# Mixture-of-experts layer: one capacity of 152 slots against eight capacities from 152 to 120, with the experts put in order on the chip

## The chip, the cores and the metric

The kernel runs on one core of a Trainium2 chip, as one program. The metric is the device time of one execution in microseconds (us). Three runs of the kernel before gave 4085.41, 4088.22 and 4089.95 us; the median is 4088.22 us. The execution that the profiler recorded took 4086.74 us.

## The reference, cut to what matters

Two transformer blocks run one after the other on 512 tokens of width 1024. The first has two layers; the second of these ends in a mixture of experts (MoE), which is the only part that changes:

```python
logits = (xt @ w_router).astype(jnp.float32)          # 512 tokens x 8 experts
top_logits, top_idx = lax.top_k(logits, TOP_K)        # TOP_K = 2
gates = jax.nn.softmax(top_logits, axis=-1)
order = jnp.argsort(top_idx.reshape(-1))              # 1024 (token, expert) pairs, sorted by expert
xs = xt[order // TOP_K]
hid = silu(ragged_dot(xs, w_gate, group_sizes)) * ragged_dot(xs, w_up, group_sizes)
ys = ragged_dot(hid, w_down, group_sizes)             # 1024 -> 3584 -> 1024 for each expert
out = einsum('nk,nkd->nd', gates, y)                  # y: ys put back into the tokens' order
```

So 1024 pairs are spread over 8 experts by the data. For the inputs of this kernel, worked out from the reference, the eight experts get 137, 118, 116, 149, 142, 117, 118 and 127 pairs (in the order of their numbers, 0 to 7).

## The kernel before

The reference's group sizes are known only at run time, while the program's shapes are fixed. So every expert gets `CAP` = 152 places ("slots") for its pairs; 8 x 152 = 1216 slots serve 1024 pairs. A fallback (`moe_overflow`) treats pairs that find no slot; it stands behind a branch on a flag, `anyo`, and is skipped if every expert's count is at most 152.

**Routing.** `moe_ranks` takes the two best experts of each token, counts with small matmuls how many earlier pairs chose the same expert (`pr`; its last row block holds the totals of the experts), and makes of it the flag and each pair's row `pos` in a buffer in DRAM (expert times 152 plus rank). `moe_route` builds expert 0's input on TensorE from a selection matrix `first`, and scatters all scaled token rows to the buffer `xg` by indirect DMAs on GpSimd.

**The expert loop** (`for e in range(NE)` in `moe`) runs the experts in the order of their numbers. For each of them `prep` loads its 152 rows (128 and 24), transposes both pieces and splits them into a rounded part and a remainder: `xhl` holds the two side by side, `xb` is a bf16 copy. Then come 14 chunks of two weight tiles each (`moe_w_gate`, `moe_w_up`, 1 MB a tile), and 16 tiles of `moe_w_down` (0.9 MB): 44 tiles an expert, 352 in all. A weight tile passes four stations (`wload_b`): a DMA issued by SP into one of five `wraw` buffers; a copy on ScalarE (ACT) to the rounded part `wh`; a subtraction on VectorE (DVE) that leaves the remainder `wl` in bf16 and frees the `wraw` buffer; and TensorE (PE), which holds 128 columns of the tile as stationary weights while the tokens stream past. There are four pairs of `wh` and `wl`. In `wh` matmuls 2 x 152 = 304 columns stream (rounded part and remainder of the tokens at once), in `wl` matmuls 152. ACT and DVE also take every result out of PSUM, on tiles of 152 or 304 columns: L935 to L946 for gate and up, L972 to L981 for down.

**The last expert** does not go through DRAM: `moe_select` makes a matrix that sends its slots to tokens, and L988 and L989 add its output to the tokens (`cb`, once for the first 128 slots and once for the other 24). At the same time GpSimd gathers the other experts' outputs and adds them (`gather_add`).

**Order.** Each engine's instruction list is put in order at build time by a scheduler that simulates the program with its own costs; tiles carry the waits. ACT, DVE and SP work off their lists in order. The weight tiles' place among the PSUM work on ACT and DVE is therefore set by that simulation, not by what the chip does.

Of the kernel before, what the change touches and what calls it, by code (L numbers as in the profile page):

```python
# [23 lines left out]
S = 512  # L24
# [4 lines left out]
CAP = 152  # L29
OVR = 384  # L30

BASE = 2 * S
HID = (8, 8, 6, 6)
# [18 lines left out]
def _constants():  # L52
# [41 lines left out]
    c["iota8"] = np.tile(np.arange(8, dtype=np.float32), (128, 1))  # L94
# [4 lines left out]
class K:  # L99
# [705 lines left out]

    def moe_begin(self, psum, h):
# [16 lines left out]
        self.iota8 = self.const("iota8", [128, 8])  # L823
# [22 lines left out]
    def moe(self, h):  # L846
        tc, nc, a = self.tc, self.nc, self.a
        C, C2 = CAP, CAP - 128
        NF = 28
        with ExitStack() as c:  # L850
# [10 lines left out]
            flags = ph.tile([1, NE * 3], I32, name="flags")  # L861
# [11 lines left out]
            def parts():  # L873
                return work.tile([128, ND, 2, C], FR, name="xhl"), work.tile([128, ND, C], BF, name="xb")
# [8 lines left out]
            def prep_first():  # L883
                x = parts()
                for d in range(ND):
                    ps = psum.tile([128, C], F, name="tr", bufs=2)
                    for t in range(NT):
                        nc.tensor.matmul(ps, h[:, t, d * 128:(d + 1) * 128], first[:, t], start=t == 0, stop=t == NT - 1)
                    split(d, ps, *x)
                return x  # L890

            def prep(e):
                xr = work.tile([128, D], F, name="xr", bufs=1)
                xr2 = work.tile([C2, D], F, name="xr2", bufs=1)
                ld = [nc.scalar.dma_start(xr, xg[BASE + e * C:BASE + e * C + 128]),
                      nc.scalar.dma_start(xr2, xg[BASE + e * C + 128:BASE + (e + 1) * C])]
# [4 lines left out]
                x = parts()  # L901
                for d in range(ND):
                    ps = psum.tile([128, C], F, name="tr", bufs=2)
                    nc.tensor.transpose(ps[:, :128], xr[:, d * 128:(d + 1) * 128], self.ident)
                    nc.tensor.transpose(ps[:, 128:], xr2[:, d * 128:(d + 1) * 128], self.ident[:C2, :C2])
                    split(d, ps, *x)
# [7 lines left out]
            for e in range(NE):  # L914
                if e == 1:
                    order.close()
                xhl, xb = nxt
                hid = [work.tile([128, n, 2, C], FR, name=f"hid{i}", bufs=1) for i, n in enumerate(HID)]
                hb = [work.tile([128, n, C], BF, name=f"hb{i}", bufs=1) for i, n in enumerate(HID)]
                at = [(i, j) for i, n in enumerate(HID) for j in range(n)]  # L920
                for ch in range(NF // 2):
                    sums = []
                    for name in ("moe_w_gate", "moe_w_up"):
                        wh, wl = ready.pop(0) if ready else self.wload_b(a[name][e, ch], 2048)
                        wh = wh.rearrange("p (d c) -> p d c", d=ND)
                        wl = wl.rearrange("p (d c) -> p d c", d=ND)
                        t = work.tile([128, 2, C], F, name=name[-4:])
# [22 lines left out]
                else:  # L950
                    sel = self.moe_select(work, psum, pos, gates, BASE + (NE - 1) * C)
                    self.gather_add(work, h, yg, pos, gates, BASE + (NE - 1) * C)
# [4 lines left out]
                yr2 = work.tile([C2, D], F, name="yr2", bufs=1)  # L957
                for d in range(ND):
                    ps = psum.tile([128, 2, C], F, name="mm", bufs=4)
                    for half in range(2):  # L960
                        wh, wl = self.wload_b(a["moe_w_down"][e, d, half], 1792)
# [9 lines left out]
                    t = work.tile([128, C], F, name="yt")  # L971
# [3 lines left out]
                    nc.tensor.transpose(pt[:, 0], t[:, :128], self.ident)  # L975
                    nc.tensor.transpose(pt[:C2, 1], t[:, 128:], self.ident)
                    ds = slice(d * 128, (d + 1) * 128)
                    y1 = work.tile([128, 2, C], F, name="w_up")[:, 0, :128] if last else yr[:, ds]
                    y2 = yr2[:, ds]
                    nc.scalar.activation(y1, pt[:, 0], AF.Copy)  # L980
                    nc.scalar.activation(y2, pt[:C2, 1], AF.Copy)  # L981
                    if last:
# [14 lines left out]
                if not last:  # L997
                    nc.scalar.dma_start(yg[BASE + e * C:BASE + e * C + 128], yr)
                    nc.scalar.dma_start(yg[BASE + e * C + 128:BASE + (e + 1) * C], yr2)
# [4 lines left out]
    def moe_select(self, work, psum, pos, gates, row0):  # L1004
        nc = self.nc
        C2 = CAP - 128
        it = self.iota_cap
# [3 lines left out]
        out = [work.tile([128, S], F, name="xr", bufs=1), work.tile([C2, S], F, name="xr2", bufs=1)]  # L1011
        for t in range(NT):
            one = [work.tile([128, CAP], F, name="yt") for _ in range(2)]
# [4 lines left out]
            nc.tensor.transpose(pt[:, 0], one[0][:, :128], self.ident)  # L1018
            nc.tensor.transpose(pt[:C2, 1], one[0][:, 128:], self.ident)
            ts = slice(t * 128, (t + 1) * 128)  # L1020
            nc.vector.tensor_copy(out[0][:, ts], pt[:, 0])
            nc.vector.tensor_copy(out[1][:, ts], pt[:C2, 1])
        return out

# [38 lines left out]
    def moe_ranks(self, pre, psum, flags, anyo, rstd, pos):  # L1063
# [14 lines left out]
        nc.vector.tensor_tensor(oh, self.iota8[:, None, None, :].to_broadcast(ohs), idf[:, :, :, None].to_broadcast(ohs),  # L1078
# [1100 lines left out]
```

## Time and profile before

| | |
|---|---|
| median of three runs | 4088.22 us |
| profiled execution | 4086.74 us |
| its span, first to last instruction | 4084.9 us |
| TensorE busy | 3862.3 us, 95% of the span |
| VectorE busy | 2884.7 us, 71% |
| ScalarE busy | 2162.8 us, 53% |
| data moved | 888.86 MB, mean 218 GB/s |
| expert loop | about 1102 to 2345 us of the span |

The shares of busy time are means over stages of very different kinds. The loop over the experts is about three tenths of the span, and it can be read by itself: windows of 148 us, cut at the starts of the experts, show each of them apart. [...] "DMA share" is the mean busy share of the 16 DMA engines.

### The profile page before, as it was taken

The page shows a single profiled execution, that of the slowest core. Times are in us where ns is not written, and L with a number is a line of the kernel's source. Part 1 is how long each engine was busy: PE and PEld are TensorE (multiplying, and loading weights), DVE is VectorE, ACT ScalarE, POOL GpSimd, SP SyncE. Part 2 cuts the span into 40 slices and gives each one's busy share as a digit, 9 for nine tenths or more (in the row PEclk, how much of TensorE's full clock was granted, in tenths as well). Part 3 has the DMA queues.
Part 4 walks back from the last instruction along what each step waited for, and adds up shares of the span by engine and source line. Part 5 has one row for each costly group of instructions (what it writes and reads, how often), then busy time and mean ns, then how long its engine had stood idle before and what let it go on. Part 6 is the DMA issues. An engine that isn't in the chain of part 4 may idle for free. (4 is left out here: it accounts for less than half of the span.)

```text
span 4084.9 us, 64628 instructions
## 1 busy us (share of the span) xinstructions
PE 3862.3 (95%) x25939; PEld 3477.4 (85%) x25940; DVE 2884.7 (71%) x4529; ACT 2162.8 (53%) x3554; POOL 605.3 (15%) x380
## 2 busy tenths in 40 slices
PE   8999999999799999999998999998889799799998
PEld 7887887999699999999997887688888799688886
DVE  4655543455388888888889658459998776677776
ACT  4332223655387777778776655533335587333333
POOL 0000000000100000000006000003444543432231
PEclk9999999999899999999999999799999899899999
DMA  4344543121489889888887521026886855899995
GB/s 135 101 135 166 186 148 107 62 77 47 161 286 321 309 298 318 306 302 311 305 303 293 189 73 57 2 104 226 292 294 233 297 185 204 311 354 335 336 338 195
DMA packets 222254, 888.86 MB, mean 218 GB/s; under 512 B 20904, under 2 KB 82105, under 8 KB 169338
## 3 DMA queue, kind: packets, MB, share of 16 engines
q1 hardware_dynamic: 102034, 640.55, 44.8%
q0 software_dynamic: 40608, 146.24, 9.9%
q10 hardware_dynamic: 79304, 97.86, 7.0%
q8 instruction: 206, 3.38, 0.3%
q14 instruction: 102, 0.84, 0.1%
HBM read 810.62 MB, written 72.38 MB: 216 GB/s over the span
## 5 line engine op out<-in xcount | busy, mean ns | idle before, releaser
L1033 DVE TENSOR_TENSOR wl<-wraw,wh 128x2048 bf16<-128x2048 f32 (+1 forms) x352 | 782.3, 2222 | 189.9 <-ACT wh L1032 188.9
L1032 ACT ACTIVATE wh<-wraw 128x2048 fp32r<-128x2048 f32 (+1 forms) x352 | 647.1, 1838 | 249.9 <-PE mm L932 118.8
L151 DVE TENSOR_TENSOR wl<-wraw,wh 128x2048 fp32r<-128x2048 f32 (+1 forms) x219 | 522.9, 2388 | 245.5 <-ACT wh L150 237.6
L150 ACT ACTIVATE wh<-wraw 128x2048 fp32r<-128x2048 f32 (+1 forms) x219 | 415.4, 1897 | 455.0 <-PE mm L157 208.9
L932 PE MATMUL mm<-xhl,wh 128*128 128x304 f32 x3584 | 617.3, 314 | 16.1 <-DVE gate L936 8.0
L932 PEld LDWEIGHTS mm<-xhl,wh 128*128 128x128 f32 x3584 | 514.9, 190 | 20.2 <-DVE w_up L936 9.6
L158 PE MATMUL mm<-xh,wl 128*128 128x384 f32 (+1 forms) x1088 | 373.6, 349 | 50.6 <-DVE wl L151 50.6
L156 PE MATMUL mm<-xh,wh 128*128 128x384 f32 (+1 forms) x1088 | 378.8, 350 | 8.4 <-ACT wh L150 6.9
L157 PE MATMUL mm<-xl,wh 128*128 128x384 f32 (+1 forms) x1088 | 378.2, 348 | 0.0
L934 PE MATMUL mm<-xb,wl 128*128 128x152 bf16 x3584 | 315.1, 231 | 0.0
L1703 POOL DMA_INDIRECT row<-in_peer_u_rows,eidx x128 | 199.3, 1557 | 694.2 <-DVE pv L1727 494.5
L157 PE MATMUL acc<-wl,ah 128*128 128x512 f32 x768 | 297.8, 397 | 1.8 <-DVE wl L151 1.8
L156 PE MATMUL acc<-wh,ah 128*128 128x512 f32 x768 | 270.0, 396 | 23.6 <-ACT ah L2013 23.6
L965 PE MATMUL mm<-hid,wh 128*128 128x304 f32 x1792 | 285.4, 309 | 0.0
L158 PE MATMUL acc<-wh,al 128*128 128x512 f32 x768 | 282.6, 397 | 0.0
L934 PEld LDWEIGHTS <-wl 128*128 128x128 bf16 x3584 | 229.2, 98 | 38.8 <-issue 0.7
L158 PEld LDWEIGHTS mm<-xh,wl 128*128 128x128 f32 x1088 | 209.7, 193 | 58.8 <-DVE wl L151 56.1
L965 PEld LDWEIGHTS mm<-hid,wh 128*128 128x128 f32 x1792 | 254.5, 189 | 0.4
L1703 POOL DMA_INDIRECT row<-in_peer_v,eidx x128 | 177.1, 1384 | 365.2 <-DVE h L1904 318.2
L156 PEld LDWEIGHTS mm<-xh,wh 128*128 128x128 f32 x1088 | 210.3, 193 | 14.1 <-ACT wh L150 8.8
L157 PEld LDWEIGHTS mm<-xl,wh 128*128 128x128 f32 x1088 | 210.3, 193 | 2.8
L156 PEld LDWEIGHTS acc<-wh,ah 128*128 128x128 f32 x768 | 145.0, 189 | 58.9 <-ACT ah L2013 23.8
(587 smaller groups left out, 8302.1 us busy)
## 6 DMA issues: line engine op xcount, KB each, us to landing
wraw<-in_moe_w_gate SPq DMA_DIRECT2D x112, 1024.0 KB
wraw<-in_moe_w_up SPq DMA_DIRECT2D x112, 1024.0 KB
wraw<-in_moe_w_down SPq DMA_DIRECT2D x128, 896.0 KB
wraw<-in_peer_u SPq DMA_DIRECT2D x64, 1024.0 KB
wraw<-in_peer_v SPq DMA_DIRECT2D x64, 1024.0 KB
wraw<-in_w_ada SPq DMA_DIRECT2D x24, 1024.0 KB
G<-gst SPq DMA_DIRECT2D x6, 4096.0 KB
gw<-G ACTq DMA_DIRECT2D x64, 384.0 KB
```

Of the source, the lines that this page charges most:

```text
L150: nc.scalar.activation(wh[:, :n], raw[:, :n], AF.Copy)
L151: nc.vector.tensor_sub(wl[:, :n], raw[:, :n], wh[:, :n].bitcast(F))
L156: mm(out, ah, bh, start=start, stop=False)
L157: mm(out, ah, bl, start=False, stop=False)
L158: mm(out, al, bh, start=False, stop=stop)
L932: nc.tensor.matmul(ps, wh[:, d, fs], xhl[:, d], start=d == 0, stop=False)
L934: nc.tensor.matmul(ps[:, 0], wl[:, d, fs], xb[:, d], start=False, stop=d == ND - 1)
L965: nc.tensor.matmul(ps, wh[:, fs], hid[at[ft][0]][:, at[ft][1]], start=ft == 0, stop=False)
L1032: nc.scalar.activation(wh[:, :n], raw[:, :n], AF.Copy)
L1033: nc.vector.tensor_sub(wl[:, :n], raw[:, :n], wh[:, :n].bitcast(F))
L1703: self.tc.keep_in_program_order(nc.gpsimd.indirect_dma_start(out=r, out_offset=None, in_=table, in_offset=bass.IndirectOffsetOnAxis(ap=eid ...
```

## The change

The eight capacities are now 152, 152, 144, 136, 132, 128, 124 and 120 (sum 1088), and belong to places in the order of work, not to experts. Expert 0 always has the first place. The other seven are put in order on the chip by their counts, the largest first, with DVE operations in `moe_ranks` that compare all counts with each other; from that come each expert's capacity and its first row. The list of experts by place (`eid`) is read by SP into registers, and from the second place on SP's weight DMAs take their address from such a register. All shapes of a place follow its capacity; places with at most 128 slots have no second piece of rows, so their second transposes and copies go, and in the last place the second half of `cb` goes. Buffers keep their sizes. The fallback gets a wider buffer and four blocks an expert instead of three; it runs only if a count is over its place's capacity. Sorted, the counts above are 137 (expert 0), 149, 142, 127, 118, 118, 117 and 116.

```diff
-CAP = 152
+CAPS = (152, 152, 144, 136, 132, 128, 124, 120)
+CAP = CAPS[0]
+START = [sum(CAPS[:i]) for i in range(NE + 1)]
...
             def prep(e):
-                xr = work.tile([128, D], F, name="xr", bufs=1)
-                xr2 = work.tile([C2, D], F, name="xr2", bufs=1)
+                C, row = CAPS[e], BASE + START[e]
+                n, C2 = min(C, 128), max(C - 128, 0)
+                xr = work.tile([128, D], F, name="xr", bufs=1)[:n]
+                ld = [nc.scalar.dma_start(xr, xg[row:row + n])]
+                if C2:
+                    xr2 = work.tile([CAP - 128, D], F, name="xr2", bufs=1)[:C2]
...
             for e in range(NE):
+                C, row = CAPS[e], BASE + START[e]
+                n1, C2 = min(C, 128), max(C - 128, 0)
+                if e:
+                    ev = nc.values_load(self.eid[0:1, e:e + 1], engines=(mybir.EngineType.SP,), min_val=0, max_val=NE - 1)
...
+                def of_expert(name, *at):
+                    if e == 0:
+                        return a[name][(0,) + at]
+                    return a[name][(bass.ds(ev, 1),) + at].rearrange("o p c -> (o p) c")
...
-                        wh, wl = ready.pop(0) if ready else self.wload_b(a[name][e, ch], 2048)
+                        wh, wl = ready.pop(0) if ready else self.wload_b(of_expert(name, ch), 2048)
-                        t = work.tile([128, 2, C], F, name=name[-4:])
+                        t = work.tile([128, 2 * CAP], F, name=name[-4:])[:, :2 * C].rearrange("p (f c) -> p f c", f=2)
...
-                            nc.tensor.matmul(ps[:, t], sel[0][:, ts], y1, start=True, stop=False)
-                            nc.tensor.matmul(ps[:, t], sel[1][:, ts], y2, start=False, stop=True)
+                            nc.tensor.matmul(ps[:, t], sel[:, ts], y1, start=True, stop=True)
...
     def moe_ranks(self, pre, psum, flags, anyo, rstd, pos):
-        fl = pre.tile([1, 3, NE], F, name="fl")
-        for q in range(3):
-            nc.vector.tensor_scalar(fl[:, q], pr[0:1, NT], float(CAP + 128 * q), None, op0=OP.is_gt)
+        key = pre.tile([128, 8], F, name="key")
+        nc.vector.scalar_tensor_tensor(key, pr[:, NT], 8.0, after, op0=OP.mult, op1=OP.add)
+        nc.vector.tensor_tensor(gt, key[:, None, :].to_broadcast(sq), key[:, :, None].to_broadcast(sq), op=OP.is_gt)
+        nc.vector.tensor_reduce(place, gt, axis=AX.X, op=OP.add)
+        nc.vector.tensor_tensor(at, i8[:, None, :].to_broadcast(sq), place[:, :, None].to_broadcast(sq), op=OP.is_equal)
+        cap, begin = pick(caps, "ecap"), pick(starts, "ebeg")
+        nc.vector.tensor_tensor(gt, at, i8[:, :, None].to_broadcast(sq), op=OP.mult)
+        nc.vector.tensor_reduce(ef, gt.rearrange("p e q -> p q e"), axis=AX.X, op=OP.add)
+        nc.vector.tensor_copy(self.eid, ef[0:1])
+        nc.vector.tensor_tensor(past, pr, cap[:, None, :].to_broadcast([128, NT + 1, 8]), op=OP.subtract)
+        fl = pre.tile([1, 4, NE], F, name="fl")
+        for q in range(4):
+            nc.vector.tensor_scalar(fl[:, q], past[0:1, NT], float(128 * q), None, op0=OP.is_gt)
...
```

Two places show what this does to the order. The first is SP's list at the start of expert 0, just behind the branch over the fallback. Before, the weight loads stand one behind the other:

```order
L868 ISA x2
L1030 DMA wraw<-in_moe_w_gate 128x2048
L1030 DMA wraw<-in_moe_w_up 128x2048
L1030 DMA wraw<-in_moe_w_gate 128x2048
L1030 DMA wraw<-in_moe_w_up 128x2048
L1030 DMA wraw<-in_moe_w_gate 128x2048
```

Now seven pairs of these rows, one pair for each later place (two pairs are shown), stand between the third and the fourth load:

```order
L874 ISA x2
L1050 DMA wraw<-in_moe_w_gate 128x2048
L1050 DMA wraw<-in_moe_w_up 128x2048
L1050 DMA wraw<-in_moe_w_gate 128x2048
L933 TENSOR_LOAD eid
L933 ISA x2
L933 TENSOR_LOAD eid
L933 ISA x2
```

So all seven register loads have moved ahead of the fourth weight load; in the later places each weight load has one more row, an `ISA`, ahead of it, for its address. The second place is DVE's list in the middle of the last expert's gate and up part, about its 21st weight tile. Before, a weight tile (`wl`) stands between the two halves of the PSUM work (`gate` or `w_up` from `mm`) of the tile before:

```order
L1033 TENSOR_TENSOR wl<-wraw,wh 128x2048
L936 TENSOR_TENSOR gate<-mm,gate 128x152
L946 TENSOR_TENSOR hid_25528<-gate,hid_25528 128x2x152
L936 TENSOR_TENSOR w_up<-mm,w_up 128x152
L1033 TENSOR_TENSOR wl<-wraw,wh 128x2048
L936 TENSOR_TENSOR w_up<-mm,w_up 128x152
L936 TENSOR_TENSOR gate<-mm,gate 128x152
L941 TENSOR_TENSOR gate<-gate,w_up 128x304
L1033 TENSOR_TENSOR wl<-wraw,wh 128x2048
```

Now it stands behind both halves of `w_up`:

```order
L1053 TENSOR_TENSOR wl<-wraw,wh 128x2048
L960 TENSOR_TENSOR w_up<-mm,w_up 128x120 x2
L965 TENSOR_TENSOR gate<-gate,w_up 128x240
L1053 TENSOR_TENSOR wl<-wraw,wh 128x2048
L960 TENSOR_TENSOR gate<-mm,gate 128x120
L970 TENSOR_TENSOR hid_26438<-gate,hid_26438 128x2x120
L960 TENSOR_TENSOR gate<-mm,gate 128x120
L1053 TENSOR_TENSOR wl<-wraw,wh 128x2048
```

Counted over the whole list, a weight tile's subtraction in a gate and up part stood 4.5 tiles ahead of the PSUM work before, in every expert. Now it stands 4.5 ahead in the places up to the fifth, 4 in the seventh, and 2 in the middle of the last one.

## Rows read from the trace of the kernel before

**Rows 1.** Windows: expert 1, then expert 7's two parts (columns as named).

```profile
core 0: us, PE busy (x) PEld busy (x) DVE busy (x) ACT busy (x) POOL busy (x), PEclk, DMA share, GB/s
1262.00:1410.00 148.00, 148.00 (x1383) 140.38 (x1381) 124.19 (x145) 115.57 (x183) 0.00 (x0) 1.00 0.88 308
2149.00:2268.00 119.00, 101.87 (x904) 93.96 (x903) 114.32 (x128) 77.94 (x128) 69.90 (x32) 0.97 0.78 283
2268.00:2336.00 68.00, 68.00 (x558) 60.67 (x556) 38.84 (x40) 46.47 (x134) 0.55 (x1) 1.00 0.49 172
```

**Rows 2.** Windows of line L932 alone: PE busy (count), PEld, clock, DMA.

```profile
1705.00:1853.00 148.00, 76.61 (x448) 64.03 (x448) 1.00 0.89 308
```

**Rows 3.** Waits, 1300 to 2000 us: total, times, longest.

```profile
DVE wl L1033 <- ACT wh L1032: 113.3, 191, 2.1
ACT wh L1032 <- PE mm L932: 73.3, 131, 0.9
```

**Rows 4.** Timeline of PE, gate and up: start, duration of the row, count.

```profile
1605.58 1.36 PE L932 MATMUL mm<-xhl,wh 128*128 128x304 f32 x8
1606.78 0.70 PE L934 MATMUL mm<-xb,wl 128*128 128x152 bf16 x8
1607.28 1.36 PE L932 MATMUL mm<-xhl,wh 128*128 128x304 f32 x8
```

**Rows 5.** Timeline of PE, another layer, 256 columns streaming.

```profile
1068.04 0.28 PE L157 MATMUL mm<-wl,nxh 128*128 128x256 f32 x1
1068.16 0.28 PE L158 MATMUL mm<-wh,nxl 128*128 128x256 f32 x1
```

**Rows 6.** Timeline of PE, the second block, 128 columns streaming.

```profile
3098.40 0.27 PE L1850 MATMUL ps<-gha,ghb 128*128 128x128 f32 x1
3098.51 0.28 PE L1851 MATMUL ps<-ghl,ghb 128*128 128x128 f32 x1
```

**Rows 7.** Timeline, the counting matmuls of the routing, then a DVE operation there.

```profile
1083.09 0.49 PE L1085 MATMUL mm<-both,low 128*128 128x8 bf16 x14 [2.29 <-DVE both L1081]
1083.85 0.20 DVE L1096 TENSOR_TENSOR oh<-oh,mm 128x64 f32<-128x64 f32 x1
```

**Rows 8.** Windows with the DMA engines nearly full, columns as in Rows 1.

```profile
2148.00:2160.00 12.00, 12.00 (x117) 11.43 (x115) 10.20 (x14) 9.00 (x15) 0.57 (x1) 1.00 0.99 357
3700.00:3800.00 100.00, 100.00 (x430) 80.48 (x429) 76.13 (x60) 31.86 (x24) 27.10 (x24) 1.00 0.96 335
```

**Rows 9.** Lines by shape, 1853 to 2000.8 us (expert 5): busy, mean ns.

```profile
L1033 DVE TENSOR_TENSOR wl<-wraw,wh 128x2048 bf16<-128x2048 f32 x29 | 66.5, 2293 | 13.3 <-ACT wh L1032 13.3
L936 DVE TENSOR_TENSOR w_up<-mm,w_up 128x152 f32<-128x152 f32 x28 | 8.7, 309 | 0.0
L941 DVE TENSOR_TENSOR gate<-gate,w_up 128x304 f32<-128x304 f32 x14 | 6.5, 468 | 0.1
L1032 ACT ACTIVATE wh<-wraw 128x2048 fp32r<-128x2048 f32 x29 | 55.6, 1917 | 17.3 <-PE mm L932 12.5 <-PE mm L965 4.9
L976 PE MATMUL tr<-c_ident,yt 128*24 128x128 f32 x9 | 2.5, 272 | 0.0
```

**Rows 10.** The same view, last expert: DVE, 2148 to 2336 us.

```profile
L1033 DVE TENSOR_TENSOR wl<-wraw,wh 128x2048 bf16<-128x2048 f32 x26 | 69.3, 2666 | 4.2 <-ACT wh L1032 4.2
L941 DVE TENSOR_TENSOR gate<-gate,w_up 128x304 f32<-128x304 f32 x14 | 13.4, 954 | 0.1
```

**Rows 11.** The same view, last expert's down part, PE, 2268 to 2336 us.

```profile
L989 PE MATMUL cb<-yr,xr 24*128 24x128 f32 x48 | 11.6, 321 | 0.0
```

**Rows 12.** Timeline of SP at the start of expert 0.

```profile
1091.96 0.33 SPq L1030 DMA_DIRECT2D wraw<-in_moe_w_gate  x1
1100.22 0.33 SPq L1030 DMA_DIRECT2D wraw<-in_moe_w_up  x1
```

**Rows 13.** Line L868, a register load: duration min/median/max in ns.

```profile
L868 SPq TENSOR_LOAD <-anyo x1: 472/472/472, 1085.1 to 1085.1; - x1
L868 SPq FUSED_REGOPS  x1: 191/191/191, 1090.3 to 1090.3; - x1
```

More of the change, by code (lines that the diff above doesn't have):

```diff
@@ L93, in _constants @@
     c["iota_cap"] = np.tile(np.arange(CAP, dtype=np.float32), (128, 1))
-    c["iota8"] = np.tile(np.arange(8, dtype=np.float32), (128, 1))
+    c["iota8"] = np.tile(np.stack([np.arange(8), CAPS, START[:8], [1e5] + [-i for i in range(1, 8)]]).astype(np.float32),
+                         (128, 1, 1)).reshape(128, 32)
     c["lowtri"] = np.concatenate([(p[:, None] < p[None, :]).astype(np.float32), np.ones((128, 128), np.float32)], 1)
@@ L860, in moe @@
             pos = ph.tile([128, 2, NT], I32, name="pos")
-            flags = ph.tile([1, NE * 3], I32, name="flags")
+            flags = ph.tile([1, NE * 4], I32, name="flags")
+            self.eid = ph.tile([1, NE], I32, name="eid")
             anyo = ph.tile([1, 1], I32, name="anyo")
@@ L950, in moe @@
                 else:
-                    sel = self.moe_select(work, psum, pos, gates, BASE + (NE - 1) * C)
-                    self.gather_add(work, h, yg, pos, gates, BASE + (NE - 1) * C)
+                    sel = self.moe_select(work, psum, pos, gates, row, C)
+                    self.gather_add(work, h, yg, pos, gates, row)
                     gf = self.bcast(work, a["final_norm_g"], D, "yr", bufs=1)
@@ L956, in moe @@
                     yr = work.tile([128, D], F, name="yr", bufs=1)
-                yr2 = work.tile([C2, D], F, name="yr2", bufs=1)
+                if C2:
+                    yr2 = work.tile([CAP - 128, D], F, name="yr2", bufs=1)[:C2]
                 for d in range(ND):
@@ L970, in moe @@
                                              stop=ft == NF - 1)
-                    t = work.tile([128, C], F, name="yt")
+                    t = work.tile([128, CAP], F, name="yt")[:, :C]
                     nc.scalar.activation(t, ps[:, 1], AF.Copy)
@@ L974, in moe @@
                     pt = psum.tile([128, 2, 128], F, name="tr", bufs=2)
-                    nc.tensor.transpose(pt[:, 0], t[:, :128], self.ident)
-                    nc.tensor.transpose(pt[:C2, 1], t[:, 128:], self.ident)
+                    nc.tensor.transpose(pt[:n1, 0], t[:, :n1], self.ident)
                     ds = slice(d * 128, (d + 1) * 128)
[L978 to L981, printed above, removed]
+                    y1 = work.tile([128, 2 * CAP], F, name="w_up")[:n1, :128] if last else yr[:n1, ds]
+                    nc.scalar.activation(y1, pt[:n1, 0], AF.Copy)
+                    if C2:
+                        nc.tensor.transpose(pt[:C2, 1], t[:, n1:], self.ident)
+                        nc.scalar.activation(yr2[:, ds], pt[:C2, 1], AF.Copy)
                     if last:
@@ L1010, in moe_select @@
         nc.vector.tensor_scalar(pf, pf, float(-row0), None, op0=OP.add)
-        out = [work.tile([128, S], F, name="xr", bufs=1), work.tile([C2, S], F, name="xr2", bufs=1)]
+        out = work.tile([128, S], F, name="xr", bufs=1)[:C]
         for t in range(NT):
-            one = [work.tile([128, CAP], F, name="yt") for _ in range(2)]
+            one = [work.tile([128, CAP], F, name="yt")[:, :C] for _ in range(2)]
             for k in range(2):
@@ L1017, in moe_select @@
             pt = psum.tile([128, 2, 128], F, name="tr", bufs=2)
[L1018 to L1022, printed above, removed]
+            nc.tensor.transpose(pt[:C, 0], one[0], self.ident)
+            nc.vector.tensor_copy(out[:, t * 128:(t + 1) * 128], pt[:C, 0])
         return out
@@ L1077, in moe_ranks @@
         oh = pre.tile(ohs, F, name="oh")
-        nc.vector.tensor_tensor(oh, self.iota8[:, None, None, :].to_broadcast(ohs), idf[:, :, :, None].to_broadcast(ohs),
+        i8, caps, starts, after = (self.iota8[:, i] for i in range(4))
+        nc.vector.tensor_tensor(oh, i8[:, None, None, :].to_broadcast(ohs), idf[:, :, :, None].to_broadcast(ohs),
                                 op=OP.is_equal)
@@ L1161, in moe_overflow @@
         with tc.For_i(0, NE, 1) as e:
-            for q in range(3):
-                rv = nc.values_load(flags[0:1, bass.ds(3 * e + q, 1)], min_val=0, max_val=1)
+            for q in range(4):
+                rv = nc.values_load(flags[0:1, bass.ds(4 * e + q, 1)], min_val=0, max_val=1)
                 with tc.If(rv > 0):
```

83 lines of the change are left out of this document (50 added, 33 removed).

## The prediction, made before the changed kernel ran

> **What bounds the kernel now.** Read first the windows cut at the starts of the experts. From the second expert to the seventh each takes about 147.5 us: such a window holds 448 of L932's matmuls, which is one expert's number [rows 2], and in it PE is busy without a break, at the upper clock level [rows 1]; the five windows that follow read alike. DVE works 124 us of it, ACT 115.5, and the DMA engines have a share of 0.88 at 308 GB/s. So PE sets this part, but the next three stand close behind it. The list of waits says the same: the weight copy on ACT mostly waits until PE has given a `wh` buffer back, and DVE waits for ACT [rows 3]. The last expert is different. While GpSimd gathers (69.9 us busy), PE works only 101.9 of 119 us and DVE 114.3 [rows 1], with every DVE operation that runs beside GpSimd lengthened: a product of 304 columns takes 954 ns there and 468 in expert 5, a weight subtraction 2666 and 2293 [rows 9, 10]. In its down part, 68 us, PE is the bound again [rows 1].
>
> The sum is made against the profiled execution, 4086.7 us; the median is 1.5 us above it, so both stand for the same.
>
> **Fewer columns on PE.** An expert has 672 matmuls with `wh` weights (448 and 224) and 672 with `wl`. From the start of one row to the start of the next, eight `wh` matmuls of 304 columns take 1.20 us and eight `wl` matmuls of 152 columns 0.50 us [rows 4]: 150 and 62 ns each, 143 of the 147.5 us; the rest is transposes and changes. What does a shorter stream cost? For `wh` the neighbours are 256 columns at 120 ns and 128 columns at 110 ns from start to start [rows 5, 6]. [...] I take 133, 125, 122, 118, 115 and 112 ns for 288, 272, 264, 256, 248 and 240 columns; the bounds at 240 are 110 and 120. For `wl` the nearest other row is 8 columns, 14 in 0.49 us, 35 ns at most [rows 7], so 120 columns lie between 35 and 62; I take them in proportion to the columns, 49.
>
> [...]
>
> Saved on PE per place, 672 times both differences: third place (144) 672 x (7 + 3.3) = 6.9 us; fourth (136) 672 x (15 + 6.5) = 14.4; fifth (132) 17.6; sixth (128) 21.4; seventh (124) 24.5. In the sixth and seventh the second pieces' transposes go too, 16 matmuls at 0.1 to 0.3 us [rows 9], some 3 us. PE would then need 140.6, 133.1, 129.9, 123.1 and 120 us.
>
> **What is late next.** The weights stay the same 44 tiles, so DMA still moves 308 GB/s x 147.5 us = 45.4 MB an expert, at a share of 0.88: 130 us of full engines. Where the engines were nearly full, they moved 357 GB/s at a share of 0.99 and 335 at 0.96 [rows 8]; these give 127 to 136 us. I take 130 as the floor of a place. DVE's 123.5 us shrink by little, since weight subtractions are most of it: PSUM operations go from 468 ns at 304 columns to 309 at 152, 1.05 ns a column [rows 9], so at 128 slots 56 operations lose 25 ns and 28 lose 50, about 3 us, to 120.5. ACT follows at 112. [...]
>
> So the third place saves 6.9, the fourth 14.4, the fifth 17.5, the sixth and the seventh 17.5 each instead of 24 to 27.5: 73.8 us together.
>
> **The last place (120 slots).** Gate and up are bound by DVE beside GpSimd, whose work stays. DVE loses 56 x 34 ns and 28 x 67 ns there, 3.8 us, a little more where they are lengthened: 119 becomes 114, if DVE stays busy. Its list now holds each subtraction back until the tile two before is out of PSUM, but PE needs 16 x (112 + 49) ns = 2.6 us for a tile and DVE 2.7 for a subtraction, so PE is in time. In the down part PE loses 224 x 41 ns = 9.2 us and half of `cb`, L989, 48 matmuls in that window with 11.6 us busy [rows 11]: 68 would become 47 to 48. ACT has 46.5 us in it and loses 7 copies of the second piece, so it comes level; I take 51. Both together save 22 us, between 8 (if ACT holds up the down part) and 28.
>
> **What is added.** Thirteen DVE operations of 8 to 64 columns stand ahead of the flag `anyo`, for which all engines wait; such an operation takes 0.2 us [rows 7], 2.6 us together, and I take 3. Queued behind them is all of the MoE. Seven register loads on SP stand between the third and the fourth weight load. One takes 0.47 us and its register work 0.22 [rows 13], 4.9 us together; SP stood idle there for 7.9 us, from 1092.3 to 1100.2, for a buffer [rows 12], and that hides them. Were that cover gone, the fourth load would come up to 5 us late, once. In the later places each weight load has 0.19 us of register work ahead of it [rows 13]; with one load in 3.35 us SP has room. The transfer itself, issued with an address from a register, does not occur in the trace; its bounds are nothing and the slow rival below, and I take nothing. The zeroing of 128 fewer rows, done far earlier, counts for nothing.
>
> **Sum:** 4086.7 - 73.8 - 22 + 3 = 3994 us.
>
> **Rivals.**
>
> (1) DMA is no floor; PE and DVE decide. For it: the share never stays at 0.99 in the expert loop, and SP always waits for buffers that DVE frees. Against it: 308 GB/s at 0.88 leaves little. The fifth, sixth and seventh place would save 17.6, 24.4 and 27 (DVE at 120.5), the last up to 28: 4086.7 - 90.3 - 28 + 3 = 3971 us. [...]
>
> (2) The gain is dampened: either `wl` does not shrink below 62 ns (third place 4.7, fourth 10.1, fifth 12.1, then the floor of 130; last 18: 4010 us), or four units that are over 0.9 busy and work in order hold each other up, so that no place gets below 136 us. Then the third saves 6.9 and the fourth to seventh 11.5 each, the last 15: 4022 us. For it: the buffers are few, five raw tiles and four split ones, and the simulated order puts subtractions later in the last two places.
>
> (3) Slower: transfers with an address from a register land late. Five raw buffers at 3.35 us a tile make a round of 16.8 us; 1.9 on ACT and 2.3 on DVE [rows 9] are taken, so a transfer may take 12.6 us before PE waits. If it takes 14, a tile takes (14 + 4.2)/5 = 3.64 us and an expert 160: seven places lose 12.5 us each, and the kernel takes some 4175 us. It is slower than before from 12.9 us on, since the last expert's savings stand against it. For it: nothing in the trace shows such a transfer. Against it: the weight loads go through the same queue of SP.
>
> (4) The counts do not fit their places, and the fallback runs. Sorted, the counts are 137, 149, 142, 127, 118, 118, 117, 116 against 152, 152, 144, 136, 132, 128, 124, 120; the narrowest margin is 2. One block of it moves 44 tiles unhidden, at least an expert's 130 us: about 4125 us.
>
> **How the numbers follow.** The forecast gets 0.47, rival 1 0.24, rival 2 0.20, rival 3 0.04, rival 4 0.01; 0.04 remain for gains that are lost altogether. 0.2% (8 us) is about what a measurement can tell from no change; faster by more gets 0.93, within it 0.03, slower 0.04. The forecast's own range is 3980 to 4008. The range runs from 3960, below rival 1 and with PE's floor of 110 ns, to 4035, above the dampened case.
>
> **What would show it.** In the profile after: matmuls of 256, 248 and 240 columns at 118 to 112 ns from start to start in their rows; the windows of the third to the seventh place 140, 133, 130, 130 and 130 us long; in the last three of them a DMA share of 0.97 or more at about 350 GB/s, PE busy but no longer without a break, and ACT waiting for `wraw` from DMA, which the waits of before do not show. A share near 0.9 with places of 120 to 123 us would be rival 1; places of 136 us with no unit full, rival 2. The last gate and up part near 114 us with DVE full, the down part near 51. The flag is read 3 us later. It is wrong if the places do not get shorter from one to the next, or if L1053's subtractions in the last place wait for PE.

## The result, and the profile after

The changed kernel takes 3988.55 us (median of four runs, 3983.97 to 3990.42); the kernel before, run beside it, 4088.75 (4085.41 to 4089.95). The ratio is 0.9755, with a 95% interval of 0.9738 to 0.9771: 100 us less. The profiled execution took 3990.42 us, with a span 96.2 us shorter than before.

First the windows, cut as those of [rows 1] at the starts of the places: the second to the seventh place, then the last one's gate and up part and its down part. Columns as there: the busy ones are microseconds in which an engine worked, with the count of its instructions in brackets, and "PEclk" is the mean granted TensorE clock of the window, 1.00 the highest value that the traces show.

```profile
1265.40:1413.20 147.80, 147.80 (x1380) 140.13 (x1377) 123.75 (x145) 114.70 (x183) 0.00 (x0) 1.00 0.87 308
1413.20:1554.90 141.70, 140.81 (x1379) 134.12 (x1377) 122.14 (x145) 114.40 (x183) 0.00 (x0) 1.00 0.87 317
1554.90:1690.50 135.60, 133.99 (x1378) 128.28 (x1377) 121.36 (x145) 112.75 (x183) 0.00 (x0) 1.00 0.93 336
1690.50:1823.00 132.50, 129.19 (x1371) 124.52 (x1369) 119.69 (x145) 110.97 (x183) 0.00 (x0) 1.00 0.93 340
1823.00:1952.30 129.30, 125.42 (x1366) 121.59 (x1364) 118.48 (x145) 108.71 (x176) 0.00 (x0) 0.99 0.95 348
1952.30:2079.20 126.90, 124.39 (x1365) 120.30 (x1363) 116.86 (x145) 107.62 (x174) 1.84 (x2) 0.99 0.92 343
2079.20:2196.20 117.00, 94.18 (x906) 89.79 (x903) 111.97 (x124) 72.29 (x124) 68.24 (x32) 0.85 0.77 292
2196.20:2241.00 44.80, 44.13 (x496) 43.23 (x493) 37.76 (x35) 39.60 (x89) 0.06 (x1) 1.00 0.80 301
```

From the second to the seventh each place is shorter than the one before it, and none stops at 130 us. From the third on PE is no longer busy without a break: it is idle for 0.9 us there, for 3.9 in the sixth and 2.5 in the seventh. DVE stays at 117 to 122 us, and the DMA share never reaches the forecast 0.97. The last gate and up part hardly gained (117.0, before 119); the down part gained most (44.8, before 68).

The pace of PE, in the timeline of the seventh place (start, duration of the row, count), answers to [rows 4]:

```profile
1990.23 1.16 PE L956 MATMUL mm<-xhl,wh 128*128 128x248 f32 x8
1991.22 0.61 PE L958 MATMUL mm<-xb,wl 128*128 128x124 bf16 x8
1991.66 1.18 PE L956 MATMUL mm<-xhl,wh 128*128 128x248 f32 x8
```

Eight matmuls of 248 columns take 0.99 us from row to row and eight of 124 columns 0.44, where 304 and 152 took 1.20 and 0.50. Taken one by one, the intervals within such rows have a median of 140 ns at 304 columns and 133, 125, 122, 118, 116 and 114 at 288 to 240; in bf16 66 at 152 and 63, 59, 60, 56, 56 and 53 at 144 to 120. Down to 240 and 120 columns they still fall.

The waits from the fifth to the seventh place (1690 to 2079 us; total, times, longest) answer to [rows 3]:

```profile
DVE wl L1053 <- ACT wh L1052: 31.6, 45, 2.4
ACT wh L1052 <- PE mm L990: 19.6, 28, 2.2
ACT wh L1052 <- PE mm L956: 11.4, 23, 0.7
PE mm L956 <- DVE gate L960: 7.0, 5, 3.0
ACT wh L1052 <- DMA wraw<-in_moe_w_gate: 5.8, 4, 2.4
```

The weight copy still waits mostly for PE. Two rows were not there before: PE waits until DVE has taken a result out of PSUM, and ACT a little for the transfer. From the third to the seventh place the waits of PE, all of them for a result that DVE had not yet taken out, make 0.9, 1.6, 3.2, 3.8 and 2.5 us, 12.0 together.

The two longest waits of this kind cost more than their own length. Here is PE in the sixth place (start, duration of the row, count):

```profile
1864.93 0.62 PE L958 MATMUL mm<-xb,wl 128*128 128x128 bf16 x8
1868.59 2.04 PE L956 MATMUL mm<-xhl,wh 128*128 128x256 f32 x8 [3.04 <-DVE gate L960]
1870.43 1.08 PE L958 MATMUL mm<-xb,wl 128*128 128x128 bf16 x8
1871.27 1.31 PE L956 MATMUL mm<-xhl,wh 128*128 128x256 f32 x8
```

```profile
1860.00:1865.00 5.00, 5.00 (x57) 4.83 (x56) 5.00 (x6) 3.48 (x5) 0.00 (x0) 1.00 0.98 347
1868.60:1871.20 2.60, 2.60 (x16) 2.51 (x17) 2.60 (x5) 0.69 (x2) 0.00 (x0) 0.50 1.02 429
```

PE stood for 3.04 us, and in the rows that follow its granted clock is 0.50, where it was 1.00 before the wait: the two rows take 2.68 us where such a pair took 1.46 just before. Until the pace is back, this costs another 1.3 us. In the seventh place the same follows a wait of 1.98 us and costs 1.6. These are the two places whose windows show a clock of 0.99; in experiments 2, 3, 6, 7 and 9 both show 1.00.

The routing and the register loads: DVE's first operation of the routing, SP's load of the flag, its seven loads of `eid`, and the third and fourth weight DMA, which answer to [rows 12, 13].

```profile
1085.66 0.17 DVE L1092 MAX8 top<-tr 128x8 f32<-128x8 f32 x1 [2.04 <-PE tr L1088]
```

```profile
L874 SPq TENSOR_LOAD <-anyo x1: 468/468/468, 1092.7 to 1092.7; - x1
```

```profile
L933 SPq TENSOR_LOAD <-eid x7: 261/275/408, 1099.7 to 1103.2; - x7
L933 SPq FUSED_REGOPS  x7: 147/147/152, 1100.0 to 1103.6; - x7
```

```profile
1099.32 0.33 SPq L1050 DMA_DIRECT2D wraw<-in_moe_w_gate  x1
1107.42 0.34 SPq L1050 DMA_DIRECT2D wraw<-in_moe_w_up  x1
```

Before, that first operation stood here:

```profile
1080.84 0.17 DVE L1072 MAX8 top<-tr 128x8 f32<-128x8 f32 x1 [2.03 <-PE tr L1068]
```

The flag is read 7.0 us after it (before 4.3, from 1080.84 to 1085.14). The loads of `eid` end 3.6 us before the fourth weight DMA is issued, 8.1 us behind the third (before 8.3): they are hidden.

Finally DVE by shape in the last place's gate and up part (busy, mean ns), which answers to [rows 10]:

```profile
L1053 DVE TENSOR_TENSOR wl<-wraw,wh 128x2048 bf16<-128x2048 f32 x26 | 75.6, 2908 | 3.0 <-ACT wh L1052 3.0
L970 DVE TENSOR_TENSOR hid<-gate,hid 128x240 fp32r<-128x240 f32 x13 | 11.9, 913 | 0.0
L965 DVE TENSOR_TENSOR gate<-gate,w_up 128x240 f32<-128x240 f32 x13 | 11.1, 855 | 0.7 <-ACT gate L962 0.2
L960 DVE TENSOR_TENSOR gate<-mm,gate 128x120 f32<-128x120 f32 x28 | 7.3, 274 | 0.0
```

A subtraction became longer (2908 ns, before 2666), and a product of 240 columns takes nearly as long as one of 304 did (855, before 954). In that part PE now waited 13.9 us, six times, for a weight subtraction; before, no wait of that kind stood in its list. An operation with one input in PSUM is not lengthened there, neither now (274 ns, last row) nor before, where it took 309 ns in expert 5 [rows 9] and in the last expert:

```profile
L936 DVE TENSOR_TENSOR w_up<-mm,w_up 128x152 f32<-128x152 f32 x28 | 8.5, 304 | 0.0
```

### The profile page after: what moved, and what is told of

It reads as the page before. It is cut to its first block, busy times and chain, and to the rows that moved or that the text cites. A ratio compares the mean times of both kernels' runs of the same rounds, so it can differ in the third digit from the quotient of the medians.

```text
span 3988.7 us, 64965 instructions
## 1 busy us (share of the span) xinstructions
PE 3737.2 (94%) x25823; PEld 3379.5 (85%) x25824; DVE 2867.6 (72%) x4540; ACT 2137.0 (54%) x3530; POOL 596.9 (15%) x380
## 5 line engine op out<-in xcount | busy, mean ns | idle before, releaser
L956 PE MATMUL mm<-xhl,wh 128*128 128x304 f32 (+6 forms) x3584 | 574.1, 304 | 20.0 <-DVE gate L960 13.7
L956 PEld LDWEIGHTS mm<-xhl,wh 128*128 128x128 f32 x3584 | 485.1, 194 | 25.7 <-DVE gate L960 9.4
L958 PE MATMUL mm<-xb,wl 128*128 128x152 bf16 (+6 forms) x3584 | 294.8, 227 | 13.9 <-DVE wl L1053 13.9
L990 PE MATMUL mm<-hid,wh 128*128 128x304 f32 (+6 forms) x1792 | 259.0, 295 | 2.1 <-DVE gate L960 2.0
L958 PEld LDWEIGHTS <-wl 128*128 128x128 bf16 x3584 | 216.0, 99 | 41.1 <-DVE wl L1053 15.1
L990 PEld LDWEIGHTS mm<-hid,wh 128*128 128x128 f32 x1792 | 232.7, 189 | 2.9 <-PE mm L958 2.4
```

The source lines that it names most:

```text
L956: nc.tensor.matmul(ps, wh[:, d, fs], xhl[:, d], start=d == 0, stop=False)
L958: nc.tensor.matmul(ps[:, 0], wl[:, d, fs], xb[:, d], start=False, stop=d == ND - 1)
L990: nc.tensor.matmul(ps, wh[:, fs], hid[at[ft][0]][:, at[ft][1]], start=ft == 0, stop=False)
```

## The experiments

Place lengths are from first to first gate matmul; the last place is counted to the start of its last weight matmul. The profiled executions reach the routing between 1076.4 and 1085.8 us (with the same code ahead of it; the kernel before at 1080.84, the changed one at 1085.66), and the part behind the experts, which no edit touches, takes 1742 to 1762 us. So a step of a few us is read from a place; the whole kernel's median carries more noise.

**1. What is added, with the last place narrow only.**

```diff
-CAPS = (152, 152, 144, 136, 132, 128, 124, 120)
+CAPS = (152, 152, 152, 152, 152, 152, 152, 120)
```

> Slots 152 in seven places and 120 in the last; the ordering on the chip and the addresses from registers stay. It gives the cost of everything that the change adds, and the last place's gain, without the narrower places three to seven. Theory (narrower streams on PE are the gain of places three to seven, and the addresses cost nothing): the places three to seven come back to the 147.6 us that they had before, so the kernel loses the 72.9 us that these places measured: about 4062 us, with the flag still read 3 us late and the last place still 162 us. Rival (transfers with an address from a register cost something that the shorter places hide): places one to six over 148 us, 4070 us or more. Rival (part of the gain of the later places came from the ordering or the addresses, not from the slots): under 4055 us.

Measured: 4054.48 us (4053.66 to 4057.25). The second to sixth place take 147.7 to 147.9 us, as before the change, with every address from a register: such transfers cost nothing here. The seventh takes 144.8, because the last place's input is prepared in it and the 8 transposes of that input's second piece are gone; the last takes 160.7. So the narrower slots are worth 66 us of the 100, the last place 26. The run is 7.5 us under the first figure and just under the second rival's 4055: 2.8 us lie in the seventh place and come with that narrower input (I had put them down to the seventh place's own slots), about 1 each lies in the first and the last place, the rest in front of the experts. Both kernels have the ordering and the addresses from registers, so none of it is theirs.

**2. Half the bytes.**

```diff
-        nc.sync.dma_start(raw[:, :n], ap)
+        nc.sync.dma_start(raw[:, :n // 2], ap[:, :n // 2])
...
+        two = raw[:, None, :n // 2].to_broadcast([128, 2, n // 2])
...
```

> Leaves out half of every expert weight: only the first half of each tile's columns is fetched, and the copies on ACT and DVE read that half twice, so that their work and PE's stay as they are and the DMA engines move half the bytes. Theory A (PE's own pace, held up a little by its neighbours, sets places four to seven; the DMA floor of 130 us that the prediction put there does not exist): places 135.6, 132.5, 129.3 and 126.9 us stay within 1.5 us, and the kernel within 4 us of 3988. Theory B (the transfers hold the fifth to seventh place up, only at a lower floor than predicted): these come down to PE's own need, which by the intervals measured in the changed kernel (672 x (122+60), (118+56), (116+56) ns plus 7 to 10 us of transposes and changes) is about 132, 125 and 122.6 us: 8 to 9 us less in these, about 3980 us or less. The last place is held by DVE and should not move by either.

Measured: 3986.48 us (3979.12 to 3990.24). Third and fourth place unchanged; the fifth to the seventh 130.8, 126.9 and 124.3, which is 1.7, 2.4 and 2.6 us less. The window of the sixth:

```profile
1817.20:1944.10 126.90, 124.69 (x1366) 120.37 (x1363) 118.16 (x145) 109.66 (x177) 0.00 (x0) 1.00 0.58 183
```

At a share of 0.58 the place is still 4 us longer than PE needs (experiment 3). Theory A is too strong and theory B mostly wrong: there is no floor of transfers here. How much of the 6.7 us in three places is the transfers' own is clean only in the fifth place (1.7). In the sixth and the seventh the clock did not fall in this run, which is worth 1.3 and 1.6 us, and the scheduler's list changed with the edit: counted as in the section on the change, in the middle of a gate and up part, the subtractions stand 4.5 tiles ahead in both, where the changed kernel has 4.3 and 4.0. The list of the last place changed too; it took 159.1 us in place of 161.6, though neither theory let it move.

**3. Half of DVE's subtraction.**

```diff
-        nc.vector.tensor_sub(wl[:, :n], raw[:, :n], wh[:, :n].bitcast(F))
+        nc.vector.tensor_sub(wl[:, :n // 2], raw[:, :n // 2], wh[:, :n // 2].bitcast(F))
...
```

> Leaves out half of the low part of every expert weight: DVE forms it for the first half of a tile's columns only, and PE uses that half twice, so that PE, ACT and the transfers have the same work and DVE loses some 1.1 us of 2.3 a tile, about 50 of 118 to 122 us a place. Theory A (DVE, which frees the raw buffers and hands PE its second weight, is what holds PE up in the places four to seven): these come down to about 134, 132, 125 and 122.6 us. Theory B (transfers): no change there within 1.5 us. Theory C (PE's own pace): no change either, and half the transfers change nothing as well. In the last place, gate and up: if DVE lengthened by GpSimd is the bound (112 of 117 us busy), it loses 26 x 1.4 us and PE's 94 us take over, 95 to 100 us in place of 117, and the kernel some 18 us less than 3988 from this alone; if PE waits there for something else, under 5 us.

Measured: 3953.41 us (3948.28 to 3959.68). The third to seventh place take 140.7, 133.7, 129.8, 122.8 and 120.6 us. Fourth to seventh:

```profile
1551.90:1685.60 133.70, 133.70 (x1380) 128.23 (x1378) 77.07 (x144) 112.01 (x183) 0.00 (x0) 1.00 0.93 338
1685.60:1815.40 129.80, 128.14 (x1372) 124.11 (x1370) 76.42 (x144) 109.70 (x182) 0.00 (x0) 1.00 0.95 345
1815.40:1938.20 122.80, 122.80 (x1367) 119.80 (x1364) 73.47 (x143) 105.84 (x175) 0.00 (x0) 1.00 0.94 351
1938.20:2058.70 120.50, 119.21 (x1362) 116.73 (x1360) 76.82 (x146) 108.88 (x174) 1.84 (x2) 1.00 0.98 370
```

With DVE light PE is busy without a break again, or nearly, and all of the bytes pass, at 370 GB/s in the seventh place. So these lengths are about PE's own need, and DVE costs PE 1.0, 1.9, 2.7, 6.5 and 6.3 us in the changed kernel, 18.4 in all, although it is idle for 10 us or more of every such place. The fall of the clock in the sixth and seventh is part of this. (The scheduler also put the subtractions nearer to their use in the sixth and seventh place here, 3.0 and 2.0 tiles ahead; in the fourth and fifth their lead is that of the changed kernel.) The last gate and up part falls to 102.9: DVE was its bound.

**4. Scaling and adding of the gathered rows on DVE.**

```diff
-                nc.gpsimd.tensor_mul(yt, yt, gates[:, k, t:t + 1].to_broadcast([128, D]))
-                nc.gpsimd.tensor_add(h[:, t], h[:, t], yt)
+                nc.vector.scalar_tensor_tensor(h[:, t], yt, gates[:, k, t:t + 1], h[:, t], op0=OP.mult, op1=OP.add)
```

> In the last place the gathered rows are scaled and added by one DVE operation of 1024 columns each (8 of them, some 1.2 us) in place of two on GpSimd (16, 2.8 and 2.7 us); GpSimd keeps the zeroing and the gathers. Theory (DVE is lengthened by GpSimd's arithmetic: its weight subtraction took 2.91 us there and 2.29 elsewhere, the products 0.88 and some 0.42, 28 us together): DVE has 112 - 28 + 10 = 94 us of work, PE's 94 us become the bound, and gate and up take 96 to 103 us in place of 117: the kernel about 3968 to 3975 us. Rival (the new operations wait in DVE's order for the gathers to land, 2 to 4 us each, with the subtractions behind them): no gain or up to 10 us lost. Rival (the lengthening has another cause than GpSimd's arithmetic): subtractions stay near 2.9 us and the kernel becomes 10 us slower.

Measured: 3977.57 us (3973.06 to 3979.56); gate and up 104.3. DVE by shape there:

```profile
L1053 DVE TENSOR_TENSOR wl<-wraw,wh 128x2048 bf16<-128x2048 f32 x26 | 59.4, 2285 | 3.5 <-ACT wh L1052 3.2 <-issue 0.2
L1079 DVE SCALAR_TENSOR_TENSOR h<-xhl,gates,h 128x1024 f32<-128x1024 f32 x8 | 10.2, 1274 | 8.4 <-DMA xhl<-yg,pos 8.4
L960 DVE TENSOR_TENSOR gate<-mm,gate 128x120 f32<-128x120 f32 x28 | 6.8, 271 | 0.0
L965 DVE TENSOR_TENSOR gate<-gate,w_up 128x240 f32<-128x240 f32 x13 | 5.2, 399 | 0.0
```

The subtractions are back at 2285 ns and the products at 399, although GpSimd's zeroing and its gathers stay: its arithmetic was what lengthened them. These are operations with both inputs in SBUF, 2908 against 2285 ns and 855 against 399; the one with an input in PSUM (L960) took 274 ns beside GpSimd's arithmetic and 271 without. The gain stopped at 13 us where 14 to 21 were expected, because DVE stood 8.4 us for the first gather (second row) and PE 9.9 us behind it.

**5. The same, in four steps** behind chosen hidden tiles, so that no gather is waited for.

```diff
...
+                with self.tc.issue_after(self.mark[(5, 7, 9, 11)[t]].ins):
                     nc.vector.scalar_tensor_tensor(h[:, t], yt, gates[:, k, t:t + 1], h[:, t], op0=OP.mult, op1=OP.add)
```

> As the kernel with scaling and adding on DVE, but the eight operations stand in DVE's order behind the 6th, 8th, 10th and 12th pair of hidden tiles of the last place, and the gathers alternate between two pairs of buffers. There DVE once stood 8.4 us for a gather to land and PE 9.9 us behind it. Theory (that wait was on the path): gate and up from 104.3 to 95 to 97 us, the kernel 7 to 9 us less than that one's 3977.6: about 3969. Rival (PE finds another wait, the subtraction's place in the order): 101 us or more, 3974 or more.

Measured: gate and up 98.7 us, so the wait was on the path; but the kernel takes 3977.98 (3971.39 to 3983.26), the same as without. The profiled execution is 5.6 us shorter in that part and 10.5 us longer behind the experts. What gives it back there is open.

**6. Narrower slots.**

```diff
-CAPS = (152, 152, 144, 136, 132, 128, 124, 120)
+CAPS = (152, 152, 144, 128, 120, 120, 120, 120)
```

> Slots 152, 152, 144, 128, 120, 120, 120, 120, which these counts still fit. PE's own need for 120 slots is, by the intervals of the changed kernel, 672 x (113 + 53) ns and 7 us of transposes and changes, 118.6 us; DVE's work is some 116. Theory (from the fourth place on DVE's work, handed on through few buffers, holds PE up by 6 us, so that a place can't get below some 125 us): fourth place 129 to 130, fifth to seventh 125 to 126 each, 16 to 18 us less than the changed kernel's 3988 in all: about 3972. Rival (PE's own pace is the limit and the 6 us go with it): fifth to seventh place 119 to 121, about 3957. Rival (these places are against a floor already): no more than 5 us.

Measured: 3955.91 us (3952.38 to 3960.63). My theory falls: DVE sets no wall of 125 us. The fourth to seventh place:

```profile
1546.20:1672.70 126.50, 124.19 (x1364) 120.21 (x1363) 117.85 (x145) 109.53 (x177) 0.00 (x0) 1.00 0.96 356
1672.70:1796.00 123.30, 119.99 (x1366) 115.79 (x1363) 116.34 (x145) 107.58 (x174) 0.00 (x0) 1.00 0.94 360
1796.00:1917.70 121.70, 119.97 (x1364) 115.34 (x1362) 112.58 (x143) 103.91 (x173) 0.00 (x0) 1.00 0.97 365
1917.70:2041.60 123.90, 119.39 (x1363) 114.13 (x1361) 116.90 (x146) 108.20 (x174) 1.85 (x2) 1.00 0.97 361
```

PE is busy for all but 2 to 5 us of these places and DVE for all but 7 to 9, and the share is 0.94 to 0.97 now. Slots still pay, 32.6 us here, and these three places stay 3 to 5 us above the 118.6 reckoned for PE.

**7. Narrower slots and half the bytes** (the edits of 2 and 6).

> Leaves out half of every expert weight (half of each tile's columns is fetched and read twice); slots 152, 152, 144, 128, 120, 120, 120, 120. With all of the bytes the fifth to seventh place took 123.3, 121.7 and 124.0 us at a DMA share of 0.94 to 0.97 and 360 to 365 GB/s; PE's own need is about 118.6 and DVE's work 113 to 117. Theory A (here the transfers are a floor, as the prediction had it, but at 121 us and not at 130): with half the bytes 118.5 to 120 us, 10 us less in the last four places together than 3955.9. Theory B (DVE's work, handed on in turns, is the limit at both): 121 to 124 us, within 4 us of 3955.9.

Measured: 3948.39 us (3932.37 to 3952.13); fifth to seventh place 122.6 each, 367.8 together where all of the bytes gave 369.0. By the places it is theory B: even at a share of 0.97 the transfers are no floor. The median is 7.5 us lower, outside theory B's 4, but only 1.2 us of it lie in the fourth to seventh place and 3.3 in the last one, and these four runs spread over 20 us. This edit changed the list as well: from the fifth to the seventh place the subtractions stand 4.5 tiles ahead, where experiment 6 has 4.0, 2.9 and 2.1.

**8. Six PSUM buffers.**

```diff
-                            ps = psum.tile([128, 2, C], F, name="mm", bufs=4)
+                            ps = psum.tile([128, 2, C], F, name="mm", bufs=6)
...
-                        ps = psum.tile([128, NT, 128], F, name="cb", bufs=2)
+                        ps = psum.tile([128, NT, 128], F, name="mm", bufs=6)
```

> Six PSUM buffers of matmul results in place of four in the expert loop (the two that only the last down part used now rotate with them); slots as in the changed kernel. Theory (PE stands because DVE, in the middle of a 2.3 us subtraction, has not yet taken a result out of PSUM: a place for two more results bridges that): fifth, sixth and seventh place from 132.5, 129.3, 126.9 to about 131, 125, 123, the kernel 6 to 10 us less than 3988. Rival (PE waits for its second weight or the work order just as long, wherever the results go): within 3 us of 3988.

Measured: 4018.73 us (4017.25 to 4024.66), 30 us worse. The third to seventh place took 140.7, 134.0, 129.9, 126.5 and 125.5 us: the fifth to the seventh gained 6.8 us where 9.7 were expected, the two before them another 2.6. But the last down part went from 44.6 to 85.6. Its longest wait:

```profile
PE tr L1000 <- DVE yt L998: 20.9, 7, 5.0
```

In DVE's list L998 of each step now stood behind the sum of the step before, which waits for PE: the two took turns.

**9. The same, the last sums in turn with the transposes** (`name="tr", bufs=2` in place of the last line above).

> Six PSUM buffers of matmul results as in the run before, slots as in the changed kernel, but the sums of the last down part take turns with its transposes in two buffers of their own, not with the matmul results. In that run the third to seventh place took 140.7, 134.0, 129.9, 126.5 and 125.5 us, and the last down part 85.6 where it had 44.6, because PE's transposes waited for a DVE operation that stood behind the sum before it. Theory (the two things are separate: two more results in PSUM save about 9 us in places two to seven, and the last down part's loss came from the shared rotation): places as there, down part 44 to 47 us, the kernel about 3978 us. Rival (the shorter places are what makes the last part worse): down part over 60 us, 3995 or more.

Measured: 3980.03 us (3974.17 to 3986.32); down part 44.6; third to seventh place 140.7, 134.0, 130.1, 126.5 and 125.5, together 9.2 us less. So two more places in PSUM bridge half of DVE's 18.4 us (with the list that the scheduler made for them). What the other half is made of was not tested apart.

**10. Six raw buffers**, with tiles of rows in and out sharing theirs.

```diff
-            self.raws += [more[0]] * 2
+            self.raws += [more[0]] * 3
...
-                    yr = work.tile([128, D], F, name="yr", bufs=1)
+                    yr = work.tile([128, D], F, name="xr", bufs=1)
```

> Six buffers of raw weights in place of five (the room comes from tiles of rows in and rows out that now share a buffer); slots as in the changed kernel. Half the bytes per tile made the fifth to seventh place 1.7, 2.4 and 2.6 us shorter. Theory (that was the time between DVE's release of a raw buffer and the next tile's arrival in it, so one buffer more does the same with all of the bytes): 131, 127, 124.5 us, the kernel 5 to 8 us less than 3988. Rival (it was the share of the DMA engines, 0.92 to 0.95, that a buffer doesn't change): within 2 us a place, the kernel within 3 us of 3988.

Measured: 4011.37 us (4009.31 to 4013.56). The fourth place gained 1.6 us, but the second lost 6.7 and the sixth 11.5, where PE waited for the rows of the next place:

```profile
PE tr L915 <- DMA xr<-xg: 8.9, 1, 8.9
```

The wait lies at the tile that was now shared, so the question of a sixth buffer stays open.

**11, 12. The savings together:** the edits of 5 and 6, and then those of 5, 6 and 9.

> Slots 152, 152, 144, 128 and 120 four times, and the last place's scaling and adding on DVE in four steps behind the hidden tiles. The two savings lie in different places: 3955.9 (slots) less the 19.5 us that the last place lost by the other (161.6 to 142.1): about 3937 us if they add up. If the kernel's part behind the experts gives some of it back, as it seemed to do for the four-step version alone (10.8 us gained by it over the changed kernel, 19.5 in its place), some 3945.

> As the kernel with the narrower slots and the four steps on DVE, with six PSUM buffers of matmul results on top, the last sums in turn with the transposes. If the two buffers save what they did at the wider slots (1 to 2.8 us a place in the second to the seventh, 9 us together), about 3928 us; less, some 3 us, if the shorter places of this kernel wait for transfers and not for PSUM: about 3935.

Measured: 3945.99 us (3941.96 to 3950.11), and 3938.82 (3937.97 to 3945.45), ratio to the kernel before 0.9648 (0.9627 to 0.9669). The first comes out at its second figure, the other 4 us above its second: the savings do not add up. The last is the best version here, 50 us under the changed kernel. Its last place takes 143.0 us (148.9 without the PSUM buffers, 142.2 in experiment 5); the fourth to seventh (126.5, 122.0, 123.3, 123.9) gain nothing from them. It fits these counts with margins of 1 to 4 slots behind the first place; other data would reach the fallback sooner.

## Why the prediction was right, and where it was not

Forecast 3994, measured 3988.55. That fewer columns on PE make the places shorter held, place by place; what holds the later places back was not what I had said:

| | predicted saving, us | measured | PE's own (experiment 3) |
|---|---|---|---|
| third | 6.9 | 6.2 | 7.2 |
| fourth | 14.4 | 12.0 | 13.9 |
| fifth | 17.5 | 15.4 | 18.1 |
| sixth | 17.5 | 18.3 | 24.9 |
| seventh | 17.5 | 21.0 | 27.3 |
| last | 22 | 25.0 | |
| routing | -3 | -2.7 | |

- **PE's columns: right.** PE alone would have saved 91.4 us in these five places by experiment 3; the predicted terms of PE, 6.9, 14.4, 17.6, 24.4 and 27.5, make 90.8. No row shows the base that they are counted from, 140 ns at 304 columns, where [rows 4] give 150; taken one by one, the intervals of both traces have a median of 140 ns there. That PE has a floor of 110 ns, as named with the range, no run shows: the `wh` matmuls went down to 114 ns at 240 columns and were still falling, and the `wl` matmuls, each with a weight load of its own, took 53 to 66. The half of rival 2 in which `wl` stays at 62 ns fails: the trace shows 56 at 128 columns.
- **The floor of 130 us from DMA: wrong.** The seventh place ran in 126.9, experiment 3 in 120.5 at 370 GB/s, and in experiment 7 places of 122 us did not get shorter with half the bytes. The failed step is "I take 130 as the floor of a place": it read the best rates of two other stretches [rows 8], 357 and 335 GB/s, as a limit.
- **DVE's part: underestimated.** I took it for hidden at 120.5 us. It costs 18.4 us. It works in order and in pieces of 2.3 us (a weight subtraction took 2291 ns on average in the sixth place), so a result in PSUM waits behind a subtraction: the list of waits shows 12.0 us of this, the falls of the clock behind the two longest add some 2.9. Two more buffers in PSUM gave 9.2 of the 18.4 back (experiment 9). For the rest the way is not shown; the release of the raw buffers, which DVE does too, is a candidate. That is the coupling of rival 2, at a smaller size. These places came out near the forecast by luck, because the two errors cancel: the floor took 17.0 us off PE's 90.8, DVE took 18.4 off 91.4.
- **Last gate and up: mis-sized** (114 predicted, 117 measured). DVE was to lose 3.8 us, "a little more where they are lengthened"; it lost 2.4 (114.3 to 112.0 us busy), since the 26 subtractions grew from 69.3 [rows 10] to 75.6 us. The lengthening belongs to GpSimd's arithmetic, not to the columns (experiment 4). Nor was "every DVE operation" beside GpSimd lengthened before: L936 was not (304 ns there, 309 in expert 5). And DVE's work alone does not give the length: in experiment 1, with the same last place, the subtractions took 69.6 us, and the part 117.2 all the same.
- **Last down part: mis-sized** (51, against 44.6). ACT did not come level (39.6 us in the window), and I counted only L989's 11.6 us [rows 11] off `cb`: with L988's 11.3 it had 22.9, and L1013, its single set now, has 6.5.
- **Routing and register loads:** 2.7 us for 3, and hidden, as predicted. Rivals 3 and 4 did not come about.
- Not forecast: the first place is 3.9 us shorter. Before, PE waited 2.7 us there for rows of the next expert; why that wait went was not tested. It does not show in the sum, as the profiled execution reached the routing 4.8 us later than the one before, with the same code ahead of it.

## What to carry to other kernels

Where several engines are nearly full (in the seventh place PE 0.98, DVE 0.92, the DMA engines 0.92), halve one engine's work at a time: what the place then takes (here 120.6 us with half of DVE's subtraction) is about the next one's own need, and the difference (6.3 us) is what the first costs, even if it shows idle time. Look whether the edit has also changed the order of the lists. A floor must be measured in the loop it is said to bound, not read from the fullest window elsewhere (130 us against 120.6 here). Part of what narrower columns saved on PE was lost where DVE, which empties PSUM, was in the middle of a subtraction of 2.3 us: 12.0 us of waits in five places, and after the two longest, 3.04 and 1.98 us, the granted clock was 0.50.

## What was not expected of the hardware

One core took 370 GB/s at a DMA share of 0.98 for 120 us (experiment 3). TensorE's granted clock was 0.50 right behind waits of 3.04 and 1.98 us, between rows at 1.00. A DVE operation with both inputs in SBUF (L965, 240 columns), 399 ns by itself in experiment 4, took 855 beside GpSimd's arithmetic, and 1024-column operations on GpSimd took from 2.1 to 3.6 us on average there, by kernel.
